# Both output projections of a two-layer decoder as seven half-size products per 1024-row chunk

## The chip, the cores and the metric

The kernel runs on one core of a Trainium2 chip. The metric is the device time of one execution in microseconds; the median of three runs of the kernel before is 1294.98 us (1292.8 to 1294.99).

## What is computed

Input and output are 1024 rows by 1024 columns of float32. The first (even) layer has two head groups, a gated linear recurrence (A, the RG-LRU) and stick-breaking attention (B). Their gated outputs stand side by side, 2048 columns, and go through one output projection. The second (odd) layer is sliding-window attention with an output projection of 1024 columns. Each layer ends with a layer norm over the residual:

```python
y = jnp.concatenate([y_a, y_b], axis=-1)              # even layer: 1024 x 2048
return jnp.einsum('bse,ed->bsd', y, w_out)            # 2048 -> 1024; odd layer: 1024 -> 1024
...
x = _layer_norm(DEEPNORM_ALPHA * x + y, ln_g[li], ln_b[li])
```

## The kernel before

Every float32 product is made of three matmuls in a reduced float32 type: both operands are split into a high and a low part, and high by high, high by low and low by high are added in PSUM (`mm3`, L109 to L112). One matmul takes a 128x128 block of the left side and moves 512 columns; PSUM holds eight banks of 128x512.

**Order.** A static scheduler fixes the order of instructions on each engine's queue when the program is built. Within a queue an instruction that waits holds up all that stand behind it; this includes SP's queue, which issues nearly all DMAs, and POOL's.

**Stages.** Even layer: attention heads with projections as filler, then the recurrence (RG-LRU, eight blocks `f`), in whose gaps the even output projection starts on the attention half of `y`; then the projection alone; then layer norm of each 128-row tile, transposes of the new `x` (`x1tr`, L626), and the odd layer's input projections (`pj_ok`, `pj_ov`, `pj_oq`, `pj_og`), its attention (`opv` is the last product of a head pair), its output projection, and the final layer norm with the stores.

**The output projection** (`out_proj`) goes over two column halves `dm`. For each it takes the pieces `e` of the contraction (16 in the even layer, 8 in the odd one, 128 rows of weight each), and for each piece the eight row tiles `s`; all eight banks accumulate at once (`ope`, `opo`). A piece is 24 matmuls. In the second half the last eight pieces run row tile by row tile, so that a row's layer norm goes beside the next row's 24 matmuls. In all there are 768 matmuls in the even layer and 384 in the odd one (its last row tile is cut in two column halves).

**Operands.** A weight piece comes by one 256 KB DMA into one of three buffers `wr`; POOL makes its high part (`wh`, L102) and its low part (`wl`, L103). Each tile of `y`, 128x1024, is split once: ACT or POOL makes the high part (L592, L590), DVE the low part (L593).

**Residual.** `xpre` holds the input rows; DVE's L492 adds a finished bank into it, L495 takes statistics. The load of `gb` (L580, 1 MB) and the eight loads of `xpre` (L582, 512 KB each) go into memory that the recurrence uses until its last product `ya` (L442).

**Layer norm.** Even: L500, L501, L505, L529 on small tiles, L531 on ACT, L532 on POOL, L537 on DVE, then the transposes with their splits L118 (ACT) and L119 (DVE). Odd: all on DVE (L500, L505, L519, L523), but for the last row.

## Time and profile before

| | |
|---|---|
| median of the three runs | 1294.98 us |
| span of the profiled execution | 1294.7 us |
| PE matmul busy | 1259.2 us (97%) |
| DVE busy | 792.5 us (61%) |
| ACT busy | 563.7 us (44%) |
| POOL busy | 566.5 us (44%) |
| instructions on PE, DVE, POOL | 6656, 1693, 695 |
| DMA | 64.15 MB, mean 50 GB/s |

Matmuls are pipelined, so the busy time of one (about 0.39 us at the full clock) is longer than the distance between the starts of two; the distance is what a matmul costs. Within a page of rows, the square bracket after an instruction is the idle time of its engine before it and what ended that.

### The profile page before, as it was taken

Reading aid. Unit: us, or ns where it says so; the run is one execution under the profiler, and the core shown is the slowest. Engines: PE = TensorE matmul, PEld = TensorE weight load, DVE = VectorE, ACT = ScalarE, POOL = GpSimd, SP = SyncE. Lnnn points to the kernel's source line nnn. Section 1 sums busy time; section 2 is a strip of 40 time slices with the busy share of each in tenths; the row PEclk is TensorE's granted clock in tenths of the full one; section 3 lists DMA queues with packets and bytes.
Section 4 is the critical chain, followed back from the end, with each engine's and each line's share of the span. In section 5 each row is a group of like instructions: output and inputs, shape, how many; then the busy total and the mean of one; then the engine's idle time right before and its main releaser. Section 6 shows DMA issues by size and latency. Waiting matters only on the chain.

```text
span 1294.7 us, 18487 instructions
## 1 busy us (share of the span) xinstructions
PE 1259.2 (97%) x6656; PEld 1077.1 (83%) x6656; DVE 792.5 (61%) x1693; ACT 563.7 (44%) x1219; POOL 566.5 (44%) x695
## 2 busy tenths in 40 slices
PE   7999999999999999999998899999999999999997
PEld 6988988898889888888776688888788888887886
DVE  6266455645564559577777931126457877778467
ACT  4134333333333335565556700013357777778400
POOL 0332243314322422556657763536445555556440
PEclk9999999999999999999999899999899999999999
DMA  6211011101110110111111052210111111111122
GB/s 204 58 41 33 25 49 34 33 17 50 33 34 24 50 37 13 37 46 46 44 49 41 25 219 64 70 29 26 49 33 33 34 34 34 33 34 40 35 90 98
DMA packets 33643, 64.15 MB, mean 50 GB/s; under 512 B 3984, under 2 KB 5392, under 8 KB 33296
## 3 DMA queue, kind: packets, MB, share of 16 engines
q1 hardware_dynamic: 32976, 61.92, 15.8%
q8 instruction: 53, 0.87, 0.3%
q10 hardware_dynamic: 576, 1.05, 0.3%
q14 instruction: 38, 0.31, 0.1%
...
## 4 chain that ended last, share of the span: by engine, by line
PE 80%; DVE 11%; ACT 4%; issue 3%; POOL 1%; DMA 1%; POOLq 0%; ACTq 0%; DVEq 0%
PE ope L110 4%; PE ope L112 4%; PE ope L111 4%; PE tr L283 2%; PE pjv L112 2%; PE pjv L111 2%; PE pjv L110 2%; PE pj_g L112 2%; PE pj_g L110 2%; PE pj_g L111 2%; PE pj_q L110 2%; PE pj_q L111 2%; PE pj_q L112 2%; PE pj_k L111 2%; PE pj_k L112 2%
## 5 line engine op out<-in xcount | busy, mean ns | idle before, releaser
L264 ACT ACTIVATE C<-z 128x512 f32<-128x512 f32 (+3 forms) x96 | 47.4, 494 | 130.2 <-DVE z L261 77.0
L756 POOL TENSOR_SCALAR S<-S,sm 128x256 f32<-128x256 f32 (+1 forms) x128 | 59.9, 482 | 77.8 <-DVE sm L754 30.0
L751 ACT ACTIVATE S<-S,sm 128x256 f32<-128x256 f32 (+1 forms) x128 | 62.6, 490 | 57.1 <-DVE sm L747 55.3
L501 ACT ACTIVATE rs<-mv,eps_t 128x1 f32<-128x1 f32 x16 | 4.7, 295 | 183.4 <-DVE mv L500 183.4
L492 DVE SCALAR_TENSOR_TENSOR xpre<-xpre,ope 128x512 f32<-128x512 f32 x16 | 10.8, 681 | 107.0 <-PE ope L112 107.0
L110 PE MATMUL pjv<-wh_v,xh 128*128 128x256 f32 x256 | 73.3, 286 | 0.0
L112 PE MATMUL pjv<-wh_v,xl 128*128 128x256 f32 x256 | 72.4, 283 | 0.0
L111 PE MATMUL pjv<-wl_v,xh 128*128 128x256 f32 x256 | 72.4, 283 | 0.0
L312 POOL TENSOR_TENSOR yb<-pvt,yb 128x128 f32<-128x128 f32 x32 | 15.8, 492 | 126.2 <-DVE pvt L311 110.0
L273 DVE TENSOR_TENSOR_SCAN C<-C,C,one 128x512 f32<-128x512 f32 x32 | 41.7, 1302 | 41.7 <-ACT C L264 41.7
L273 DVE TENSOR_TENSOR_SCAN C<-C,one 128x512 f32<-128x512 f32 (+1 forms) x64 | 54.7, 854 | 16.4 <-ACT C L264 16.3
L118 ACT CAST wt<-tr 128x512 fp32r<-128x512 f32 (+3 forms) x96 | 46.6, 486 | 40.7 <-PE tr L283 38.9
L275 DVE TENSOR_TENSOR B<-B,C 128x512 f32<-128x512 f32 (+3 forms) x96 | 57.3, 597 | 10.2 <-ACT pvt L309 0.5
L261 DVE TENSOR_TENSOR z<-z,mask 128x128 f32<-128x128 f32 x64 | 18.8, 296 | 67.6 <-PE z L259 65.7
L102 POOL TENSOR_SCALAR wh_g<-wr_g 128x512 fp32r<-128x512 f32 x16 | 10.7, 668 | 111.3 <-PE pjv L112 42.6
L110 PE MATMUL pj_k<-xh,wh_k 128*128 128x512 f32 x128 | 52.7, 412 | 5.6 <-DVE wh_k L105 5.6
L119 DVE TENSOR_TENSOR wt<-tr,wt 128x512 fp32r<-128x512 f32 (+3 forms) x96 | 52.6, 549 | 7.9 <-ACT wt L118 7.6
L110 PE MATMUL pj_ag<-xh,wh_ag 128*128 128x512 f32 x128 | 51.8, 405 | 5.7 <-DVE xc L381 5.7
L110 PE MATMUL ope<-wh_e,yhb 128*128 128x512 f32 x128 | 51.2, 403 | 6.2 <-DVE gg L395 3.8
L110 PE MATMUL pj_oq<-x1h,wh_oq 128*128 128x512 f32 x128 | 52.8, 412 | 0.0
L111 PE MATMUL pj_k<-xl,wh_k 128*128 128x512 f32 x128 | 51.2, 400 | 1.3 <-DVE xl L133 1.3
L110 PE MATMUL pj_q<-xh,wh_q 128*128 128x512 f32 x128 | 52.0, 406 | 0.1
...
## 6 DMA issues: line engine op xcount, KB each, us to landing
...
```

The lines of the kernel that those rows point to most:

```text
L110: nc.tensor.matmul(ps, wh, xh, start=start, stop=False)
L111: nc.tensor.matmul(ps, wh, xl, start=False, stop=False)
L112: nc.tensor.matmul(ps, wl, xh, start=False, stop=stop)
L118: nc.scalar.copy(h, ps)
L119: nc.vector.tensor_tensor(out=l, in0=ps, in1=h.bitcast(F32), op=ALU.subtract)
L261: nc.vector.tensor_tensor(out=z[:, W - P:W], in0=z[:, W - P:W], in1=mask, op=ALU.add)
L264: nc.scalar.activation(C[:, :W], z[:, :W], AF.Sigmoid, scale=-SC)
L273: nc.vector.tensor_tensor_scan(cr, cr, one.broadcast_to([P, W]), init, ALU.mult, ALU.mult)
L275: nc.vector.tensor_tensor(out=B[:, :W], in0=B[:, :W], in1=C[:, 1:W + 1], op=ALU.mult)
L283: nc.tensor.transpose(tr[:, t * P:(t + 1) * P], B[:, t * P:(t + 1) * P], ident)
L751: nc.scalar.activation(Sb[:, j, lo:], Sb[:, j, lo:], AF.Exp, bias=nm[:, j:j + 1], accum_out=den[:, j:j + 1])
L756: nc.gpsimd.tensor_scalar(out=Sb[:, j, lo:], in0=Sb[:, j, lo:], scalar1=rec[:, j:j + 1], scalar2=0.0, op0=ALU.mult, op1=ALU.add)
```

## The change

`out_proj` gives way to `fast_out`. The contraction is cut into chunks of 1024 (even: the attention half first, then the recurrence half; odd: one). Each chunk is a 2x2 block product with blocks of 512, done as seven block products instead of eight (a Strassen form). A product is four row tiles by four 128-row pieces by three, 48 matmuls, in four banks; two sets of four banks alternate (X and Y). P0 is A11 by B11 (X), P1 A12 by B21 (Y), P2 S2 by T2 (added on P0's banks), P3 S1 by T1 (Y), P4 S3 by T3 (X), P5 S4 by B22 (on Y), P6 A22 by T4 (on X).

DVE adds each product into one to three quarters of `xpre` (`add_to`, L502 and L504 of the new file). The sums S of quarters of `y` are formed by DVE (L571), the sums T of weight quarters by POOL (L571), from weights that are loaded again for each product (L593). Splits are made per product and per 128x512 tile, one product ahead in the program text: `y` high on ACT (L622), low on DVE (L623), weight high on ACT (L626; before on POOL), weight low on POOL (L627). The last chunk's P5 finishes row tiles 0 to 3, and P6 finishes 4 to 7, each followed by its layer norm; the cut of the last odd row goes away. L549 and L554 are the old L532 and L537. PE's queue holds 6086 matmul and transpose rows against 6252.

```diff
+    XB = ["pj", "pj", "pj", "pv"]
+    YB_ = ["z", "z", "tr", "tr"]
 
     LNC = 768
 
-    def out_proj(w_src, es, yh, n_tail, tail_piece, lnp, gb, after, name, final):
+    PRODUCTS = [("A11", "B11", 0, True), ("A12", "B21", 1, True), ("S2", "T2", 0, False), ("S1", "T1", 1, True),
+                ("S3", "T3", 0, True), ("S4", "B22", 1, False), ("A22", "T4", 0, False)]
+    def fast_out(w_src, chunks, lnp, wtmp, wop, gb, after, name, final, first_by_rows):
...
+        def add_to(half, dm, p, ps, cols=(0, HALF)):
+            s = half * 4 + p
             c0, c1 = cols
             xt = xpre[:, s, dm * HALF + c0:dm * HALF + c1]
+            if (s, dm, c0) in touched or (s, dm, 0) in touched:
+                nc.vector.tensor_tensor(out=xt, in0=ps[:, c0:c1], in1=xt, op=ALU.add)
+            else:
+                nc.vector.scalar_tensor_tensor(out=xt, in0=xt, scalar=ALPHA, in1=ps[:, c0:c1],
+                                               op0=ALU.mult, op1=ALU.add)
+            touched.add((s, dm, c0))
...
+            def y_raw(op, t):
+                if op in ("A11", "A12", "A22"):
+                    return {"A11": A11, "A12": A12, "A22": A22}[op][t]
+                if op == "S2":
+                    if "S2" not in hold:
+                        hold["S2"] = half_tiles(f"S2{pre}")
+                    tt(nc.vector, A11[t], A11[t], A21[t], ALU.subtract)
+                    tt(nc.vector, hold["S2"][t], A22[t], A11[t], ALU.subtract)
+                    return hold["S2"][t]
+                if op == "S1":
+                    tt(nc.vector, A21[t], A21[t], A22[t], ALU.add)
+                    return A21[t]
+                if op == "S3":
+                    return A11[t]
+                if op == "S4":
+                    tt(nc.vector, A12[t], A12[t], hold["S2"][t], ALU.subtract)
+                    return A12[t]
+            def w_load(j, k, t, nm):
+                raw = wpool.tile([P, HALF], F32, tag="wr", name=f"wr_{nm}{pre}_{t}", bufs=3)
+                nc.sync.dma_start(raw, w_src[j, e0 + 4 * k + t])
+                return raw
+            def w_raw(op, t):
+                if op in ("B11", "B21", "B22"):
+                    return w_load(int(op[2]) - 1, int(op[1]) - 1, t, op)
+                if op == "T2":
+                    if "T2" not in hold:
+                        hold["T2"], hold["T3"] = half_tiles(f"T2{pre}"), half_tiles(f"T3{pre}")
+                    b22, b12 = w_load(1, 1, t, "c"), w_load(1, 0, t, "d")
+                    tt(nc.gpsimd, hold["T3"][t], b22, b12, ALU.subtract)
+                    b11 = w_load(0, 0, t, "e")
+                    tt(nc.gpsimd, hold["T2"][t], hold["T3"][t], b11, ALU.add)
+                    return hold["T2"][t]
+                if op == "T3":
+                    return hold["T3"][t]
+                if op == "T1":
+                    b12, b11 = w_load(1, 0, t, "f"), w_load(0, 0, t, "g")
+                    tt(nc.gpsimd, b12, b12, b11, ALU.subtract)
+                    return b12
...
+            def make(i, t):
+                yop, w_op = PRODUCTS[i][:2]
+                r = y_raw(yop, t)
+                yo_ = slot(f"yo{pre}{i}_{t}", F32R)
+                nc.scalar.copy(yo_[:, 0, :], r)
+                nc.vector.tensor_tensor(out=yo_[:, 1, :], in0=r, in1=yo_[:, 0, :].bitcast(F32), op=ALU.subtract)
+                r = w_raw(w_op, t)
+                wh, wl = wop(f"{pre}{i}_{t}")
+                nc.scalar.copy(wh, r)
+                nc.gpsimd.tensor_tensor(out=wl, in0=r, in1=wh.bitcast(F32), op=ALU.subtract)
+                return yo_, wh, wl
...
+        def mm(ps, ops, p, t, start, stop, c0=0, c1=HALF):
+            yo_, wh, wl = ops
+            c = slice(p * P, (p + 1) * P)
+            f = partial(nc.tensor.matmul, skip_group_check=True)
+            f(ps[:, c0:c1], yo_[:, 0, c], wh[:, c0:c1], start=start, stop=False)
+            f(ps[:, c0:c1], yo_[:, 0, c], wl[:, c0:c1], start=False, stop=False)
+            f(ps[:, c0:c1], yo_[:, 1, c], wh[:, c0:c1], start=False, stop=stop)
...
+        prep(0)
+        for k, (ci, i) in enumerate(steps):
+            prep(k + 1)
+            ops = made.pop(k)
...
+            if last and i >= 5:
+                half = i - 5
+                for p in range(4):
+                    s = half * 4 + p
+                    b = ps[xy, p]
+                    for t in range(4):
+                        mm(b, ops[t], p, t, False, t == 3)
+                    dm = 1 - half
+                    add_to(half, dm, p, b)
+                    stat(s, dm, 0, HALF)
+                    mr = ln_a(s)
+                    if pend is not None:
+                        ln_c(pend)
+                    ln_b(s, *mr)
+                    pend = s
                 continue
+            if fresh:
+                for p in range(4):
+                    ps[xy, p] = bank(tags[p], f"fo{name}{ci}_{i}_{p}")
+            rows = first_by_rows and k == 0
+            order_ = [(p, t) for p in range(4) for t in range(4)] if rows else \
+                [(p, t) for t in range(4) for p in range(4)]
+            for p, t in order_:
+                mm(ps[xy, p], ops[t], p, t, fresh and t == 0, t == 3)
+            for p in range(4):
+                b = ps[xy, p]
+                for half, dm in ([(0, 0)], [(0, 0)], [(0, 1), (1, 0), (1, 1)], [(1, 1)], [(1, 1)],
+                                 [(0, 1)], [(1, 0)])[i]:
+                    add_to(half, dm, p, b)
+                    if last and ((i == 1) or (i == 4)):
+                        stat(half * 4 + p, dm, 0, HALF)
...
+    def wop_pool(nm):
+        return (wpool.tile([P, HALF], F32R, tag="wh", name=f"wh_{nm}", bufs=5),
+                wpool.tile([P, HALF], F32R, tag="wl", name=f"wl_{nm}", bufs=5))
+    fast_out(w_even_out, [([ytile["b", n] for n in range(8)], 8), ([ytile["a", f] for f in range(8)], 0)],
+             lnp, None, wop_pool, gb, after_even, "e", False, False)
...
+    def wop_slot(nm):
+        hl = slot(f"whl_{nm}", F32R)
+        return hl[:, 0, :], hl[:, 1, :]
+    fast_out(w_odd_out, [([ytile["o", p] for p in range(8)], 0)], ep, None, wop_slot, gb2, after_odd, "o", True, True)
```

Three places show how the order moves. The first is SP's queue at the end of the recurrence. Before, three weight pieces of the even projection, then the loads of `gb` and `xpre`, then the next piece:

```order
L93 DMA wr_e_0_7258<-in_w_even_out_dram 128x512
L93 DMA wr_e_1_7288<-in_w_even_out_dram 128x512
L93 DMA wr_e_2_7318<-in_w_even_out_dram 128x512
L580 DMA gb<-in_e_ln_dram 128x2048
L582 DMA xpre<-in_x_dram 128x1024 x8
L93 DMA wr_e_3_7348<-in_w_even_out_dram 128x512
```

Now (the letters c, d, e are the three quarters of which T3 and T2 are formed, f and g those of T1; the digit is the 128-row piece):

```order
L593 DMA wr_ee_1_7108<-in_w_even_out_dram 128x512
L593 DMA wr_ce_2_7120<-in_w_even_out_dram 128x512
L593 DMA wr_de_2_7122<-in_w_even_out_dram 128x512
L693 DMA gb<-in_e_ln_dram 128x2048
L695 DMA xpre<-in_x_dram 128x1024 x8
L593 DMA wr_ee_2_7125<-in_w_even_out_dram 128x512
L593 DMA wr_ce_3_7137<-in_w_even_out_dram 128x512
L593 DMA wr_de_3_7139<-in_w_even_out_dram 128x512
L593 DMA wr_ee_3_7142<-in_w_even_out_dram 128x512
L593 DMA wr_fe_0_7209<-in_w_even_out_dram 128x512
L593 DMA wr_ge_0_7211<-in_w_even_out_dram 128x512
```

The third load of piece 2 of T2 now stands behind the nine loads, and with it all of piece 3 and T1. The second place is POOL's queue over the same weights. Before, each piece is one copy and one subtraction:

```order
L102 TENSOR_SCALAR wh_e_3_7350<-wr_e_3_7348 128x512
L103 TENSOR_TENSOR wl_e_3_7351<-wr_e_3_7348,wh_e_3_7350 128x512
L102 TENSOR_SCALAR wh_e_4_7380<-wr_e_4_7378 128x512
L103 TENSOR_TENSOR wl_e_4_7381<-wr_e_4_7378,wh_e_4_7380 128x512
L102 TENSOR_SCALAR wh_e_5_7410<-wr_e_5_7408 128x512
```

Now, for the products P2 (T2) and P3 (T1, which is formed in the tile wr_fe):

```order
L627 TENSOR_TENSOR wl_e_1_7112<-T2e_7082,wh_e_1_7111 128x512
L571 TENSOR_TENSOR T3e_7085<-wr_ce_2_7120,wr_de_2_7122 128x512
L571 TENSOR_TENSOR T2e_7083<-T3e_7085,wr_ee_2_7125 128x512
L571 TENSOR_TENSOR T3e_7085<-wr_ce_3_7137,wr_de_3_7139 128x512
L571 TENSOR_TENSOR T2e_7083<-T3e_7085,wr_ee_3_7142 128x512
L571 TENSOR_TENSOR wr_fe_0_7209<-wr_fe_0_7209,wr_ge_0_7211 128x512
L627 TENSOR_TENSOR wl_e_2_7129<-T2e_7083,wh_e_2_7128 128x512
L627 TENSOR_TENSOR wl_e_3_7146<-T2e_7083,wh_e_3_7145 128x512
```

The low part of P2's piece 2 now stands behind the sums of piece 3 and the first sum of T1. The third place is the end of the even projection, on POOL. Before, five rows' L532 stand behind the last weight piece in one group:

```order
L102 TENSOR_SCALAR wh_e_7_7803<-wr_e_7_7801 128x512
L103 TENSOR_TENSOR wl_e_7_7804<-wr_e_7_7801,wh_e_7_7803 128x512
L532 TENSOR_TENSOR xpre<-xpre,gb 128x1024 x5
L102 TENSOR_SCALAR whl_ok_8175<-wr_ok_8173 128x512
L102 TENSOR_SCALAR whl_ok_8180<-wr_ok_8178 128x512
```

Now, with the weights of the last product P6 (T4, formed in T2's tiles):

```order
L627 TENSOR_TENSOR wl_e_0_8206<-T2e_7776,wh_e_0_8205 128x512
L571 TENSOR_TENSOR T2e_7777<-wr_he_3_8232,T2e_7777 128x512
L549 TENSOR_TENSOR xpre<-xpre,gb 128x1024 x2
L627 TENSOR_TENSOR wl_e_1_8216<-T2e_7776,wh_e_1_8215 128x512
L627 TENSOR_TENSOR wl_e_2_8226<-T2e_7777,wh_e_2_8225 128x512
L627 TENSOR_TENSOR wl_e_3_8236<-T2e_7777,wh_e_3_8235 128x512
L549 TENSOR_TENSOR xpre<-xpre,gb 128x1024 x2
```

Two rows' L549 now stand ahead of the low parts of three of the four pieces of the last product.

## Rows read from the trace of the kernel before

**Rows 1.** Busy time of each engine in stretches, granted clock, DMA share.

```profile
core 0: us, PE busy (x) PEld busy (x) DVE busy (x) ACT busy (x) POOL busy (x), PEclk, DMA share, GB/s
...
720.00:740.00 20.00, 15.15 (x50) 11.58 (x51) 20.00 (x15) 15.99 (x18) 14.06 (x9) 0.83 0.13 41
740.00:905.00 165.00, 165.00 (x746) 136.97 (x745) 53.35 (x83) 20.82 (x29) 84.44 (x70) 1.00 0.25 80
...
1215.00:1275.00 60.00, 59.73 (x266) 49.46 (x267) 35.13 (x62) 4.54 (x9) 22.46 (x24) 1.00 0.22 71
```

**Rows 2.** Timeline of PE: start, duration, instruction; the odd layer's first projections.

```profile
911.98 0.80 PE L110 MATMUL pj_ov<-x1h,whl_ov 128*128 128x512 f32 x1 [1.87 <-POOL whl_ov L102]
...
914.28 0.63 PE L110 MATMUL pj_oq<-x1h,wh_oq 128*128 128x512 f32 x1
914.71 0.63 PE L111 MATMUL pj_oq<-x1l,wh_oq 128*128 128x512 f32 x1
```

**Rows 3.** Timelines of DVE, SP and POOL at the end of the recurrence.

```profile
754.00 0.92 DVE L442 TENSOR_TENSOR ya<-xc,gg 128x512 f32<-128x512 f32 x1
...
755.00 0.33 SPq L580 DMA_DIRECT2D gb<-in_e_ln_dram  x1
...
760.84 0.33 SPq L93 DMA_DIRECT2D wr_e<-in_w_even_out_dram  x1
...
771.91 0.62 POOL L102 TENSOR_SCALAR wh_e<-wr_e 128x512 fp32r<-128x512 f32 x1 [11.07 <-DMA wr_e<-in_w_even_out_dram]
```

**Rows 4.** Groups by line, POOL 700 and DVE 740 to 905 us: busy, mean ns, idle.

```profile
L532 POOL TENSOR_TENSOR xpre<-xpre,gb 128x1024 f32<-128x1024 f32 x7 | 16.9, 2411 | 21.7 <-ACT xpre L531 21.6
...
L495 DVE BATCH_NORM_STATS2 ste<-xpre 128x6 f32<-128x512 f32 x16 | 10.8, 687 | 0.2
L492 DVE SCALAR_TENSOR_TENSOR xpre<-xpre,ope 128x512 f32<-128x512 f32 x16 | 10.8, 681 | 107.0 <-PE ope L112 107.0
L537 DVE TENSOR_TENSOR xpre<-xpre,gb 128x1024 f32<-128x1024 f32 x7 | 9.0, 1280 | 0.1
L119 DVE TENSOR_TENSOR x1l<-x1tr,x1h 128x512 fp32r<-128x512 f32 x8 | 5.3, 668 | 0.0
L593 DVE TENSOR_TENSOR yhla<-ya,yhla 128x1024 fp32r<-128x1024 f32 x1 | 1.2, 1211 | 0.0
```

**Rows 5.** Timeline of POOL in the undisturbed stretch of the even projection.

```profile
819.93 1.29 POOL L103 TENSOR_TENSOR wl_e<-wr_e,wh_e 128x512 fp32r<-128x512 f32 x1
...
823.95 0.62 POOL L102 TENSOR_SCALAR whl_e<-wr_e 128x512 fp32r<-128x512 f32 x1 [0.46 <-DMA wr_e<-in_w_even_out_dram]
```

**Rows 6.** Timeline of SP: the load into the buffer freed at 821.22 us.

```profile
821.25 5.04 SPq L93 DMA_DIRECT2D wr_e<-in_w_even_out_dram  x3
```

**Rows 7.** Timeline of DVE, end of the even projection: additions of three of eight rows.

```profile
864.95 0.69 DVE L492 SCALAR_TENSOR_TENSOR xpre<-xpre,ope 128x512 f32<-128x512 f32 x1 [1.48 <-PE ope L112]
870.39 0.69 DVE L492 SCALAR_TENSOR_TENSOR xpre<-xpre,ope 128x512 f32<-128x512 f32 x1 [1.84 <-PE ope L112]
...
901.18 0.69 DVE L492 SCALAR_TENSOR_TENSOR xpre<-xpre,ope 128x512 f32<-128x512 f32 x1 [2.33 <-PE ope L112]
```

**Rows 8.** Timeline of PE: the last product of the odd attention.

```profile
1219.86 0.28 PE L787 MATMUL opv<-ptl,VP 128*128 128x256 f32 x1
```

**Rows 9.** Timeline of DVE: additions of two rows before the final layer norm, last instruction.

```profile
1255.14 0.68 DVE L492 SCALAR_TENSOR_TENSOR xpre<-xpre,opo 128x512 f32<-128x512 f32 x1
...
1259.68 0.68 DVE L492 SCALAR_TENSOR_TENSOR xpre<-xpre,opo 128x512 f32<-128x512 f32 x1
...
1290.35 0.96 DVE L523 SCALAR_TENSOR_TENSOR xpre<-xpre,rs,gb 128x384 f32<-128x384 f32 x1
```

**Rows 10.** Timelines of POOL and DVE in the recurrence, where both read SBUF tiles.

```profile
719.04 1.71 POOL L103 TENSOR_TENSOR wl_e<-wr_e,wh_e 128x512 fp32r<-128x512 f32 x1
720.72 1.59 POOL L102 TENSOR_SCALAR wh_e<-wr_e 128x512 fp32r<-128x512 f32 x1
...
719.54 2.28 DVE L593 TENSOR_TENSOR ylb<-yb,yhb 128x1024 fp32r<-128x1024 f32 x1
```

108 lines of the change are left out of this document (33 added, 75 removed).

## The prediction

> **What bounds the kernel now.** I read the windows by stage first. From 740 to 905 us, the even output projection, PE is busy all the time at the full clock, DVE a third of it; from 1215 to 1275 us, the odd one, PE is busy for 59.73 of 60 us [rows 1]. The cost of a matmul at the full clock is read from the row tiles at the end of the even projection: 24 matmuls between two additions that wait for PE, 5.44 us, 0.2267 each [rows 7]. At the half clock, which PE showed after 1.87 us of idling, two matmuls start 0.43 us apart [rows 2]. So in both projections the number of matmuls sets the time, and whoever takes matmuls away gains, as long as operands come in time. Third, the places where PE could starve. At the end of the recurrence DVE is the full engine (20.00 of 20 us, PE 15.15) [rows 1], and a weight piece behind the loads of `gb` and `xpre` keeps POOL waiting for 11.07 us [rows 3]. PE doesn't feel that, because it has pieces in hand. At the ends of the two layers, DVE and POOL follow the last matmuls [rows 7, 9].
>
> **Matmuls removed.** Seven products of 48 instead of eight: 48 matmuls per chunk, three chunks. Even: 96 x 0.2267 = -21.8 us; odd: 48 x 0.2267 = -10.9 us [rows 7]. That is -32.7 us if nothing else moves.
>
> **Start of the even projection.** Call L the end of the recurrence's last product, 754.92 us [rows 3]. By then PE had done some 133 of the 768 `ope` matmuls: from L to the last row's addition at 901.18 [rows 7] it was never idle [rows 1]; 146.3 us hold 645 matmuls, less some ten for the transposes that stand between. In the new order P0, P1 and two pieces of P2 can be done by L: 120, much the same. But the third load of P2's piece 2 stands behind the loads of `gb` and `xpre` on SP, where before stood a piece that PE didn't need yet. These loads can't start before L (755.00), and what is behind them reached POOL at 771.91, L + 17.0 [rows 3]. Then POOL's queue: the T2 sum of piece 2 (1.29 us, a subtraction's time [rows 5]) to L + 18.3; T3 of piece 3 to L + 19.6; the load of its third quarter into the buffer freed at L + 18.3, which takes 2.73 us (a buffer freed at 821.22 was used at 823.95 [rows 5, 6]), to L + 21.0; T2 of piece 3 to L + 22.3; the two loads of T1 into buffers freed at L + 19.6, to L + 22.4; T1 to L + 23.7; and only then the low part of piece 2, to L + 25.0. PE stands from about L to L + 25.0. With the 13 matmuls by which it is behind (2.9) and one piece of 12 at the half clock (12 x 0.20 = 2.4) it lags by 30.3. L itself can move: DVE, the full engine, makes fewer splits of `y` before L (six of 1.21 less would be 7 us [rows 4]), but sums S come in. Bounds -1 and +7, I take 2.5 us earlier. Term: **+27.8** (20 to 32).
>
> **Operands in the other products.** Before, POOL worked one copy and one subtraction (L102 0.62, L103 1.29 [rows 5]) per 24 matmuls, 1.91 us in 5.44. Now a piece feeds 12 matmuls, 2.72 us. A plain piece needs one subtraction, 1.29, and is covered. A piece of T2 needs three operations, 3.87 us, and three loads in three buffers, so that from one T3 to the next at least 1.29 + 2.73 = 4.02 us pass; a piece of T1 has two loads and the same 4.02. For the eight pieces that is 8 x (4.1 - 2.72) = 11 us of PE waiting if nothing was made ahead, and 0 if all was. In the second even chunk some can be made during P0 and P1, where POOL needs half of the time: I take 6. The same banks serve P6 of one chunk and P0 of the next, so that PE waits for additions (0.68 each [rows 4]): 1. Term: **+7** (2 to 12).
>
> **End of the even layer.** On POOL two L549, 2.41 us each [rows 4], now stand ahead of the low parts of three pieces of P6, the last product: +3 (2 to 5). Since these pieces come last, the four rows 4 to 7 end together, where before a row ended every 5.44 us and its layer norm lay beside the next one's matmuls. Before, the first `pj_ov` matmul came 10.8 us after the last row's addition [rows 2, 7]. Now DVE has, from the last matmul to that point, 4 additions (2.7), 4 statistics (2.8), 12 transposed splits (8.0), 5 final additions L554 (6.4) [rows 4], and a dozen instructions of a few columns, between 0 and half of a 128x512 one each (0 to 4, I take 3): 22.9, and with the first transposes and ACT's casts 24.1. The projections `pj_ok` lie in it before and after. +13.3 (5 if the rows still end one by one, to 16). Even layer in all: -21.8 + 27.8 + 7 + 3 + 13.3 = **+29**.
>
> **Odd layer.** The last attention product ends at 1220.1 [rows 8]. Before, 294 matmuls were left, covered by PE alone. Now 24 of P0 and P1 and five products are left, 264, 59.8 us of PE. The sums of T2 need slots that P0 gives free: POOL starts on them at about 1223. Nothing is made ahead here, so T2 and T1 go at their own pace: 8 x 4.1 = 33 us, 1256; the last low part and 12 matmuls, 1260; P4 (10.9), 1271. From there DVE sets the end: P4's additions and statistics and some splits stand ahead, 4 x (0.68 + 0.69) + 2 = 7.5 [rows 4]; then eight rows' layer norm. A row costs DVE 4.54 us back to back (1255.14 to 1259.68 [rows 9]); before, most of the eight lay beside 5.44 us of matmuls each, now a row has only 12 matmuls (2.72), and the eight take 8 x 4.54 = 36.3. After DVE's last instruction (1291.31 [rows 9]) 3.4 us of stores follow. End: 1271 + 7.5 + 36.3 + 3.4 = 1318, against 1294.7: **+23.5**, the 10.9 us of removed matmuls included. Lower bound: no wait for operands, P4 ends at 1220 + 168 x 0.2267 = 1258, additions hidden but for 2.7: 1258 + 2.7 + 36.3 + 3.4 = 1300.5, +6. Upper: POOL at the contended times of [rows 10], +30. POOL's and ACT's split instructions for P0 and P1 also stand among the last attention heads' steps, which can move the attention's end by -3 to +10; I take 0.
>
> **Sum.** 1294.7 + 29 + 23.5 = 1347.2 us of span; the median is 0.3 above the span. Forecast 1347.5 us. All lower ends give 1294.7 + 7 + 3 = 1305, all upper ones 1294.7 + 43 + 40 = 1378.
>
> **Rivals.**
> 1. *POOL and DVE exclude each other.* In the recurrence a POOL subtraction began at 719.04 and took 1.71; DVE's split began at 719.54 and took 2.28 instead of 1.21, ending 1.07 after POOL's end; POOL's copy, begun at 720.72, took 1.59 instead of 0.62, that is until 0.5 after DVE's end [rows 4, 10]. They went one after the other. A chunk now has 44 POOL operations (44 x 1.29 = 56.8) and 44 DVE ones from SBUF (half of 1.21 to 0.68, 28.6): 85.4 us one after the other, against 336 x 0.2267 = 76.1 of PE. In the first chunk +9, in the second +4 beyond my 6, and a T2 piece of the odd chunk at 5.2 instead of 4.1, 4 x 1.1: +17, 1364.5 us. Against it: both engines have slack in the plain products, and T2's pace is set by loads that no engine delays. The Trainium skill (SBUF — State Buffer, "SBUF: two separate sides") has this as a rule: the port pair that the two share is an exclusive lock, held for a whole instruction by whichever starts first, for DVE instructions with two SBUF inputs. The rows above agree.
> 2. *Only the start costs.* P2's and P3's sums run ahead of PE in the second chunk and the odd layer, and the last even rows end one by one: -21.8 + 27.8 + 2 + 2 + 5 = +15, odd +6: 1316 us.
> 3. *Faster.* The recurrence ends early enough. DVE and POOL are its full engines, and the change takes copies off POOL (to ACT) and whole-tile splits off DVE. If L came 20 us sooner, the start's term would be 10; with every other cost at its lower end, -21.8 + 10 + 2 + 2 + 5 = -3, odd +6 - 3: 1295 us. It decides from 23 us on, and at 30 would give 1285. For it: DVE has no free time there [rows 1]. Against: six splits fewer are 7 us, and the gates' chain remains.
> 4. *The removal doesn't take place.* PE's queue is 166 rows shorter; I give it nothing.
>
> **How the numbers follow.** Forecast (1325 to 1357) 0.56; rival 1 and other upper ends (above 1357) 0.16; rival 2 (1298 to 1325) 0.20; within 0.2%, about what a measurement of this kernel tells from no change, 0.02; faster 0.06. So slower 0.92. The range 1306 to 1368 leaves out faster and same (0.08), some 0.06 of rival 2 and 0.06 above.
>
> **What would show it.** Right: PE stands still for 20 us or more in one piece just after the loads of `gb` and `xpre`, POOL waits there for the piece behind them; in the last even product four rows' additions follow each other on DVE; in the odd layer POOL's T2 sums come every 4 to 5 us with PE waiting for them, and DVE has no gap from P4 to the end. The start is wrong if PE's longest gap there is under 15 us; the odd term is wrong if P4 ends before 1262 us less the shift of what stands ahead; all is wrong if the second even chunk and both ends run at PE's pace of 2.72 us a piece.

## The result, and the profile after

The changed kernel takes 1359.89 us (median of four runs, 1359.33 to 1361.2); the kernel before took 1294.04 us beside it (1292.8 to 1294.99). The ratio is 1.0515, with a 95% interval of 1.050 to 1.053: slower by 5%. The profiled execution has a span of 1357.6 us against 1294.7. Two single runs among the experiments, one of the two of e5 and one of the eight of e8, took some 80 us more than the same kernel's others and are left out. Times are medians of a kernel's runs (of two for most experiments); landmarks inside the span come from one profiled execution. The length of a product runs from the start of the first of its 48 matmuls to the start of the next product's first, counted in PE's order.

The page of the changed kernel, its first part (busy time, share of the span, instructions) and, from the second, PE and its granted clock in 40 slices of 33.9 us:

```profile
PE 1248.7 (92%) x6488; PEld 1056.3 (78%) x6488; DVE 943.7 (70%) x1876; ACT 637.7 (47%) x1368; POOL 650.1 (48%) x724
...
PE   8999999999999999999996399797999999998793
...
PEclk9999999999999999999999699897999999998897
```

PE carries out fewer matmuls and has lost its full share in slices 22 and 23 (713 to 781 us, the start of the even projection), 26 (848 to 882, its second chunk), 28 (916 to 950, the end of the even layer), and 37, 38 and 40 (the odd projection and the end). DVE is now busy for 943.7 us, before for 792.5. The windows that answer to [rows 1], with the busy time of each engine and the instructions in brackets:

```profile
core 0: us, PE busy (x) PEld busy (x) DVE busy (x) ACT busy (x) POOL busy (x), PEclk, DMA share, GB/s
720.00:740.00 20.00, 16.00 (x61) 12.54 (x62) 20.00 (x20) 10.79 (x14) 13.09 (x8) 0.91 0.19 54
740.00:786.00 46.00, 18.79 (x53) 13.81 (x52) 34.42 (x37) 16.29 (x29) 24.40 (x15) 0.63 0.56 200
...
832.00:922.00 90.00, 78.53 (x336) 63.33 (x334) 63.19 (x83) 29.71 (x51) 66.36 (x44) 0.94 0.32 97
922.00:950.00 28.00, 18.49 (x77) 13.52 (x77) 25.94 (x38) 13.26 (x22) 20.01 (x13) 0.76 0.09 29
...
1263.00:1312.00 49.00, 39.26 (x146) 27.90 (x147) 40.98 (x45) 17.64 (x32) 38.19 (x26) 0.93 0.41 128
1312.00:1357.00 45.00, 21.81 (x96) 17.52 (x94) 42.07 (x79) 8.20 (x17) 14.70 (x11) 0.78 0.31 111
```

Between 740 and 905 us PE was never idle before [rows 1]. Now it gets through 53 matmuls in the 46 us to 786, where the full pitch of 0.2267 us would have given 203.

| landmark, us | before | after | difference |
|---|---|---|---|
| recurrence's last product ends (L) | 754.92 | 751.67 | -3.3 |
| last row's addition / last even matmul ends | 901.2 | 921.9 | +20.7 |
| first `pj_ov` matmul | 911.98 | 949.96 | +38.0 |
| last attention product | 1220.1 | 1257.4 | +37.3 |
| end of the span | 1294.7 | 1357.6 | +62.9 |

**Start of the even projection.** PE's gaps (the idle time before an instruction and its releaser stand in the square bracket), then POOL's queue, SP's, and a row of DVE's in the same stretch:

```profile
758.74 0.77 PE L635 MATMUL foe<-wh_e,yoe 128*128 128x512 f32 x1 [17.79 <-DVE xpre L504]
771.39 2.07 PE L635 MATMUL foe<-wh_e,yoe 128*128 128x512 f32 x4 [4.41 <-ACT wh_e L626]
778.48 0.79 PE L636 MATMUL foe<-wl_e,yoe 128*128 128x512 f32 x1 [5.02 <-POOL wl_e L627]
```
```profile
751.09 1.71 POOL L571 TENSOR_TENSOR T3e<-wr_ce,wr_de 128x512 f32<-128x512 f32 x1
767.55 3.14 POOL L571 TENSOR_TENSOR T2e<-T3e,wr_ee 128x512 f32<-128x512 f32 x1 [14.75 <-DMA wr_ee<-in_w_even_out_dram]
770.65 1.26 POOL L571 TENSOR_TENSOR T3e<-wr_ce,wr_de 128x512 f32<-128x512 f32 x1
773.29 1.26 POOL L571 TENSOR_TENSOR T2e<-T3e,wr_ee 128x512 f32<-128x512 f32 x1 [1.38 <-DMA wr_ee<-in_w_even_out_dram]
775.49 1.27 POOL L571 TENSOR_TENSOR wr_fe<-wr_fe,wr_ge 128x512 f32<-128x512 f32 x1 [0.94 <-DMA wr_ge<-in_w_even_out_dram]
776.71 3.40 POOL L627 TENSOR_TENSOR wl_e<-T2e,wh_e 128x512 fp32r<-128x512 f32 x2
```
```profile
751.75 0.33 SPq L693 DMA_DIRECT2D gb<-in_e_ln_dram  x1
752.17 4.48 SPq L695 DMA_DIRECT2D xpre<-in_x_dram  x8
757.85 0.33 SPq L593 DMA_DIRECT2D wr_ee<-in_w_even_out_dram  x1
```
```profile
764.07 5.50 DVE L623 TENSOR_TENSOR yoe<-yb,yoe 128x512 fp32r<-128x512 f32 x9
```

The loads of `gb` and `xpre` leave right after L. The third quarter of P2's piece 2 (`wr_ee`) stands behind them and reaches POOL at L + 15.9, where 17.0 had been worked out from [rows 3]. Then comes the queue that the prediction wrote down: T2, T3, T2, T1 and only then the low part of piece 2. It begins at 776.71, L + 25.0; the prediction had its end there. PE has it at 778.48, L + 26.8. The main cause is the first T2 sum, 3.14 us instead of 1.29: DVE's splits follow each other every 0.60 us until 769.57, and the sum ends 1.1 us behind the last of them. What else the prediction had otherwise is the first gap. It let pieces 0 and 1 of P2 run before L. P2 accumulates on P0's banks, P0's additions into `xpre` wait for the loads of `xpre`, and so these pieces too came after them; PE stood from 740.95, before L.

**Second even chunk, its P2.** POOL's rows, one of SP's, then PE's two longest gaps:

```profile
856.60 1.68 POOL L571 TENSOR_TENSOR T3e<-wr_ce,wr_de 128x512 f32<-128x512 f32 x1 [1.72 <-DVE yoe L623]
858.36 1.60 POOL L571 TENSOR_TENSOR T2e<-T3e,wr_ee 128x512 f32<-128x512 f32 x1
861.87 1.60 POOL L571 TENSOR_TENSOR T3e<-wr_ce,wr_de 128x512 f32<-128x512 f32 x1 [1.90 <-DMA wr_de<-in_w_even_out_dram]
863.54 1.59 POOL L571 TENSOR_TENSOR T2e<-T3e,wr_ee 128x512 f32<-128x512 f32 x1
867.15 1.46 POOL L571 TENSOR_TENSOR wr_fe<-wr_fe,wr_ge 128x512 f32<-128x512 f32 x1 [2.02 <-DMA wr_ge<-in_w_even_out_dram]
868.57 1.71 POOL L627 TENSOR_TENSOR wl_e<-T2e,wh_e 128x512 fp32r<-128x512 f32 x1
```
```profile
858.69 0.43 SPq L593 DMA_DIRECT2D wr_de<-in_w_even_out_dram  x1
```
```profile
861.89 1.19 PE L635 MATMUL foe<-wh_e,yoe 128*128 128x512 f32 x4 [2.87 <-ACT wh_e L626]
870.33 0.80 PE L636 MATMUL foe<-wl_e,yoe 128*128 128x512 f32 x1 [7.25 <-POOL wl_e L627]
```

From one T3 to the next it is 861.87 - 856.60 = 5.27 us. The prediction had 4.02 at least: a sum of 1.29 and a load of 2.73. The sum took 1.68, 0.39 more, as the others take 1.6 here where a subtraction alone took 1.29 [rows 5]. The larger part, 0.86, is the load: T3 needs two quarters, both leave when T3's end frees their buffers (858.31 and 858.69), and the second could be used 3.59 us after that end. P2 took 23.0 us instead of 10.88. (The expectations of e4 and e7 give 22.4 for it, some three matmuls too few.)

**End of the even layer.** DVE's and POOL's rows from the last matmuls on, and the first projection matmul of the odd layer:

```profile
920.11 3.38 DVE L554 TENSOR_TENSOR xpre<-xpre,gb 128x1024 f32<-128x1024 f32 x1 [2.38 <-POOL xpre L549]
...
937.51 3.41 DVE L554 TENSOR_TENSOR xpre<-xpre,gb 128x1024 f32<-128x1024 f32 x1 [1.35 <-POOL xpre L549]
...
943.67 3.42 DVE L554 TENSOR_TENSOR xpre<-xpre,gb 128x1024 f32<-128x1024 f32 x2
```
```profile
935.03 4.80 POOL L549 TENSOR_TENSOR xpre<-xpre,gb 128x1024 f32<-128x1024 f32 x2 [7.99 <-ACT xpre L548]
...
945.97 3.34 POOL L549 TENSOR_TENSOR xpre<-xpre,gb 128x1024 f32<-128x1024 f32 x1
```
```profile
949.96 0.50 PE L110 MATMUL pj_ov<-x1h,whl_ov 128*128 128x512 f32 x1
```

From the last matmul (921.9) to `pj_ov` it takes 28.1 us, before 10.8 [rows 2, 7]. L554 cost 1.28 in [rows 4]; beside POOL the four shown took 3.4, 3.4 and twice 1.7. POOL's last layer norm products come as late as 935 to 949, because the four rows end together.

**Odd projection.** POOL's and DVE's queues while P3 ends and P4 runs, and DVE from there to its last instruction:

```profile
1299.11 6.95 POOL L627 TENSOR_TENSOR whl_o<-T3o,whl_o 128x512 fp32r<-128x512 f32 x4
1306.02 6.93 POOL L627 TENSOR_TENSOR whl_o<-wr_B22o,whl_o 128x512 fp32r<-128x512 f32 x4
```
```profile
1306.03 7.47 DVE L623 TENSOR_TENSOR yoo<-yo,yoo 128x512 fp32r<-128x512 f32 x5
```
```profile
1303.00:1354.00 51.00, 30.81 (x136) 24.96 (x134) 50.97 (x89) 11.93 (x24) 23.01 (x16) 0.84 0.29 101
```

P4 ends at 1311.7, which is 54.4 us after the attention's last product; the prediction had 51. One load was not priced: that of the odd layer norm's constants (1 MB) leaves on SP at 1261.07, ahead of a quarter of T2's second piece at 1262.99, and POOL has that quarter only at 1269.41, 6.4 us later. The two columns that matter in the last row are the third (DVE, 50.97 of 51 us) and the first (PE, 30.81): after P4 DVE alone sets the end, as forecast.

### The profile page after: what moved, and what is told of

Same layout as the page of the kernel before. It is cut to its first block, busy times and chain, and to the rows that moved or that the text cites. A ratio compares the mean times of both kernels' runs of the same rounds, so it can differ in the third digit from the quotient of the medians.

```text
span 1357.6 us, 18732 instructions
## 1 busy us (share of the span) xinstructions
PE 1248.7 (92%) x6488; PEld 1056.3 (78%) x6488; DVE 943.7 (70%) x1876; ACT 637.7 (47%) x1368; POOL 650.1 (48%) x724
## 4 chain that ended last, share of the span: by engine, by line
PE 65%; DVE 17%; POOL 6%; ACT 4%; DMA 3%; issue 3%; POOLq 0%; SPq 0%; ACTq 0%; DVEq 0%
PE tr L283 2%; PE pjv L112 2%; PE pjv L110 2%; PE pjv L111 2%; PE pj_g L112 2%; PE pj_oq L110 2%; PE pj_g L110 2%; PE pj_oq L112 2%; PE pj_oq L111 2%; PE pj_g L111 2%; PE pj_q L110 2%; PE pj_q L112 2%; PE pj_q L111 2%; PE pj_k L111 2%; PE pj_k L112 2%
## 5 line engine op out<-in xcount | busy, mean ns | idle before, releaser
L635 PE MATMUL foe<-wh_e,yoe 128*128 128x512 f32 x224 | 82.8, 410 | 30.8 <-DVE xpre L504 17.8
L264 ACT ACTIVATE C<-z 128x512 f32<-128x512 f32 (+3 forms) x96 | 47.5, 495 | 130.2 <-DVE z L261 77.0
L636 PE MATMUL foe<-wl_e,yoe 128*128 128x512 f32 x224 | 91.5, 409 | 14.4 <-POOL wl_e L627 14.4
L842 POOL TENSOR_SCALAR S<-S,sm 128x256 f32<-128x256 f32 (+1 forms) x128 | 58.8, 474 | 78.7 <-DVE sm L840 33.6
L637 PE MATMUL foe<-wh_e,yoe 128*128 128x512 f32 x224 | 90.2, 405 | 0.0
L635 PEld LDWEIGHTS foe<-wh_e,yoe 128*128 128x128 f32 x224 | 43.7, 197 | 43.4 <-issue 20.1
L273 DVE TENSOR_TENSOR_SCAN C<-C,C,one 128x512 f32<-128x512 f32 x32 | 41.7, 1303 | 41.7 <-ACT C L264 41.7
L636 PEld LDWEIGHTS foe<-wl_e,yoe 128*128 128x128 f32 x224 | 44.6, 199 | 25.7 <-POOL wl_e L627 16.4
L275 DVE TENSOR_TENSOR B<-B,C 128x512 f32<-128x512 f32 (+3 forms) x96 | 57.4, 597 | 10.2 <-ACT pvt L309 0.5
L102 POOL TENSOR_SCALAR wh_g<-wr_g 128x512 fp32r<-128x512 f32 x16 | 10.7, 666 | 110.4 <-PE pjv L112 42.5
L502 DVE TENSOR_TENSOR xpre<-foe,xpre 128x512 f32<-128x512 f32 x56 | 36.5, 683 | 33.7 <-PE foe L637 33.2
```

The lines of the kernel that those rows point to most:

```text
L264: nc.scalar.activation(C[:, :W], z[:, :W], AF.Sigmoid, scale=-SC)
L273: nc.vector.tensor_tensor_scan(cr, cr, one.broadcast_to([P, W]), init, ALU.mult, ALU.mult)
L275: nc.vector.tensor_tensor(out=B[:, :W], in0=B[:, :W], in1=C[:, 1:W + 1], op=ALU.mult)
L635: f(ps[:, c0:c1], yo_[:, 0, c], wh[:, c0:c1], start=start, stop=False)
L636: f(ps[:, c0:c1], yo_[:, 0, c], wl[:, c0:c1], start=False, stop=False)
L637: f(ps[:, c0:c1], yo_[:, 1, c], wh[:, c0:c1], start=False, stop=stop)
```

## The experiments

Kernels e1 to e7 are edits of the changed kernel, e8 and e9 rearrange its even part, e10 and e11 are edits of the kernel before. Line numbers of an edited kernel are shifted by a few.

**e1: the even layer in the new form, the odd one in the old.** `out_proj` stands beside `fast_out`, and only the call at the odd layer's end changes:

```diff
-    fast_out(w_odd_out, [([ytile["o", p] for p in range(8)], 0)], ep, None, wop_slot, gb2, after_odd, "o", True, True)
+    out_proj(w_odd_out, list(range(8)), yh_odd, 8, lambda ti, src, nm: load_piece(src, nm, pool=slots),
+             ep, gb2, after_odd, "o", True)
```

> The even projection in the new form, the odd one as before. My theory, that the two projections cost separately: the even one ends 38.0 us later than before in the changed kernel's trace (first pj_ov product 911.98 before, 949.97 after), so about 1294 + 38 = 1332 us. Rival, that the costs are shared (for instance the odd layer's attention pays for what the even one leaves behind): more than 3 us away from 1332.

Measured: 1333.15 us, ratio 1.0309 (1.0279 to 1.0339). The two layers' costs add up: the odd one costs 1359.9 - 1333.2 = 26.7 us (predicted 23.5), the even one the rest, some 40 (predicted 29). 1333.15 lies 1.2 us from the 1332 of the expectation.

**e2: the odd layer's sums T from six buffers of their own**, so that no load waits for a buffer:

```diff
-                raw = wpool.tile([P, HALF], F32, tag="wr", name=f"wr_{nm}{pre}_{t}", bufs=3)
+                if final and nm in "cdefgh":
+                    raw = lnp.tile([P, HALF], F32, tag="wr2", name=f"wr_{nm}{pre}_{t}", bufs=6)
+                else:
+                    raw = wpool.tile([P, HALF], F32, tag="wr", name=f"wr_{nm}{pre}_{t}", bufs=3)
```

> The changed kernel, but the odd projection's quarters for T2, T1 and T4 are loaded into six buffers of their own instead of the three shared ones. Theory (three buffers and the load's way into them set the pace of T2 and T1): the eight pieces of P2 and P3, 37.9 us from 1263.7 to 1301.5 us in the changed kernel, fall to about 30, and the kernel gains 4 to 8 us, less than the pieces do, because DVE has work of its own there. Rival (POOL and DVE exclude each other, POOL's own time sets the pace): pieces stay above 35 us, the kernel gains under 2 us.

Measured: 1359.93 us, ratio 1.0516 (1.0479 to 1.0552): no gain. The waits for loads did go. P2 and P3 together took 33.6 us instead of 37.2 (the expectations have 37.9, up to P3's last matmul, with four of P4's in between). But see what POOL and DVE did in the meantime (timeline of e2, POOL first, then DVE):

```profile
1272.95 3.43 POOL L571 TENSOR_TENSOR T3o<-wr_co,wr_do 128x512 f32<-128x512 f32 x2
1276.34 3.42 POOL L571 TENSOR_TENSOR T2o<-T3o,wr_eo 128x512 f32<-128x512 f32 x2
```
```profile
1273.46 3.46 DVE L571 TENSOR_TENSOR S2o<-yo,yo 128x512 f32<-128x512 f32 x2
1276.85 3.46 DVE L571 TENSOR_TENSOR yo<-yo,S2o 128x512 f32<-128x512 f32 x2
```

Neither engine idles, and each needs 1.7 us for an operation of two SBUF inputs: one of POOL, one of DVE, one of POOL. DVE's splits for P4 came later, P4 took 16 us instead of 10.9, and the gain was gone. My theory named the loads as what sets T2's pace; they were one of two limits that lay over each other.

**e3: the even layer's loads in the order of their need.** The quarter of `xpre` that P0 adds into goes first on SP (1 MB), the other 3 MB (`rest`) go on ACT's queue, and `gb` comes after the first chunk's last weights:

```diff
-    nc.sync.dma_start(gb, ...)
-    for s in range(NS):
-        nc.sync.dma_start(xpre[:, s, :], x[s * P:(s + 1) * P, :])
+    for s in range(4):
+        nc.sync.dma_start(xpre[:, s, 0:HALF], x[s * P:(s + 1) * P, 0:HALF])
...
+            if k == 1 and not final:
+                rest()
+            if k == 5 and not final:
+                load_gb(wdma[0, 'B22', 3])
```

> The changed kernel, but of the residual only the quarter that P0 and P1 are added to is loaded on SP ahead of the weights (1 MB); the other 3 MB go by ACT's queue, and the layer norm's constants (1 MB) after the first chunk. Theory (what stands still at the start are the 5 MB ahead of the weights on SP): the third load of T2's piece 2 reaches POOL 6 to 10 us after the end of the recurrence instead of 15.9, P3 of the first chunk ends 5 to 12 us earlier, the kernel gains as much. Rival (POOL's queue of sums, 44 operations a chunk, is the cause): under 2 us.

Measured: 1354.96 us, ratio 1.0477 (1.0447 to 1.0508); the span is 4.6 us shorter than that of the changed kernel and `pj_ov` comes 5.3 us earlier. POOL's wait, which was 14.75 us:

```profile
760.76 1.42 POOL L572 TENSOR_TENSOR T2e<-T3e,wr_ee 128x512 f32<-128x512 f32 x1 [7.69 <-DMA wr_ee<-in_w_even_out_dram]
```

This is L + 10.2 instead of L + 15.9, and the 5 us arrive at the end of the span. The three marks of the theory (6 to 10 us to POOL, P3's end and the kernel 5 to 12 us earlier) are each missed by a little, the last two with 4.9; the rival, under 2 us, is out. So the loads ahead of the weights are a cause of the start's cost, though not all of it: PE's first gap is still 15.75 us.

**e4: the low part of `y` isn't made.** In both projections the third matmul uses the high part instead, so that DVE does 84 operations less:

```diff
-                nc.vector.tensor_tensor(out=yo_[:, 1, :], in0=r, in1=yo_[:, 0, :].bitcast(F32), op=ALU.subtract)
...
-            f(ps[:, c0:c1], yo_[:, 1, c], wh[:, c0:c1], start=False, stop=stop)
+            f(ps[:, c0:c1], yo_[:, 0, c], wh[:, c0:c1], start=False, stop=stop)
```

> The changed kernel without the splits that make the low part of y in both projections; the third matmul takes the high part again, so PE's work is the same and the result is not the reference's. DVE loses 84 instructions with two SBUF inputs, 51 us at 0.61 each. Theory (loads and queue order): POOL's operations get back to about 1.29 us, but the waits of P2 in the second even chunk (22.4 us for 48 matmuls) and of the odd P2 and P3 (37.9 us) stay within 3 us of that; the kernel gains 6 to 12 us, nearly all at the odd end, where DVE is full. Rival (exclusion of POOL and DVE sets these waits): both fall by 4 us or more, the kernel gains 18 us or more.

Measured: 1336.47 us, ratio 1.0334 (1.0304 to 1.0364), 23.4 us less. POOL's subtractions were back to 1.29 us wherever DVE had no sum beside them. In the places that the expectation names, less happened than the rival said: P2 of the second chunk took 3.3 us less (19.7; the theory had allowed 3), P2 and P3 of the odd layer 0.6 less (36.6). But the gain is far beyond the 6 to 12 us of the theory, and most of it lies elsewhere than at the odd end. L comes at 742.04, 9.6 us earlier, since DVE is the full engine of the recurrence [rows 1], and the splits for P0 and P1 stand in its queue there. The windows row of e4 for the recurrence's end shows DVE (third column) at 14.48 of 20 us, where it had been 20.00:

```profile
720.00:740.00 20.00, 16.21 (x59) 12.28 (x59) 14.48 (x13) 14.24 (x18) 11.29 (x9) 0.87 0.22 69
```

`pj_ov` is 14.7 us earlier, the attention's end 19.5 us. This bears on the prediction's third rival: L does move when DVE has less to do, but 9.6 us is what leaving out all these splits gives, and the rival needs 23.

**e5: e2 and e4 together** (diffs as above).

> The two edits of e2 and e4 together: the odd projection's quarters in six buffers of their own, and no low part of y (the high part is used twice, so the result is not the reference's). Theory (two limits of nearly the same height lie over each other in the odd projection: the load into three buffers, and the time in which POOL and DVE keep each other out; taking away one shows the other): with both gone the eight pieces of P2 and P3 go at POOL's own pace, 4 x 3.87 + 4 x 2.58 = 26 us, so 26 to 30 us after 37.9 in the changed kernel, 33.6 in e2 and 36.4 in e4, and the time is 4 to 9 us under e4's 1336.5. Rival (the buffers matter nowhere, as e2's time alone says): within 2 us of e4's.

Measured: 1331.42 us, 5.1 less than e4. In the odd layer P2 and P3 take 31.6 us, not the 26 to 30 expected; P2 to P4 take 42.5 us. The changed kernel took 48.1 for P2 to P4, e2 49.5, e4 47.5. Either remedy alone gives 0.6 us or nothing, both give 5.6. That is the mark of two limits one behind the other: loads into three buffers, and DVE's splits. POOL's row for the same two sums that took 3.42 us in e2:

```profile
1256.44 2.48 POOL L571 TENSOR_TENSOR T2o<-T3o,wr_eo 128x512 f32<-128x512 f32 x2
```

DVE has nothing to do there, and POOL needs 1.2 us a sum. So the two engines do hold each other up. How much of the 5.6 us is that, and how much the splits' own time in DVE's queue, these runs don't separate: without the splits both are gone.

**e6: the second half of every odd row's layer norm on ACT and POOL**, as the last row has it already:

```diff
-            if final and s == NS - 1:
+            if final:
+                cut = LNC if s == NS - 1 else HALF
...
-                edges = (0, LNC // 2, LNC) if s == NS - 1 else (0, 512, 1024)
+                edges = (0, LNC // 2, LNC) if s == NS - 1 else (0, HALF)
```

> The changed kernel, but the second half of each row tile's last layer norm goes by ACT and POOL, as that of the last row's end did already. DVE's work per row falls from 4.54 to 3.1 us. Theory (from the end of P4 on DVE alone sets the end, 45.2 us): the end comes 3 to 9 us sooner; nearer 4 if POOL's two products per row (1.29 each) keep DVE's with two SBUF inputs out, nearer 9 if they run side by side. Rival (the stores or PE set the end): under 1 us.

Measured: 1361.98 us, ratio 1.0536 (1.0506 to 1.0567), no gain; from P4's end to the span's end 45.9 us, before 45.8 (the expectation has 45.2). DVE has 14 operations of 0.74 us fewer and seven of one column more, and from P4's end to its last instruction it idles for 0.07 us in all; POOL ends 1.8 us behind it. So neither the stores nor PE set the end. Its remaining operations beside POOL (timeline of e6, DVE, then POOL):

```profile
1343.00 0.74 DVE L541 SCALAR_TENSOR_TENSOR xpre<-xpre,rs,gb 128x512 f32<-128x512 f32 x1
1343.66 1.75 DVE L537 SCALAR_TENSOR_TENSOR xpre<-xpre,mv,gb 128x512 f32<-128x512 f32 x1
...
1346.65 1.76 DVE L541 SCALAR_TENSOR_TENSOR xpre<-xpre,rs,gb 128x512 f32<-128x512 f32 x1
```
```profile
1343.14 1.72 POOL L532 TENSOR_TENSOR xpre<-xpre,gb 128x512 f32<-128x512 f32 x1
1344.82 1.71 POOL L531 TENSOR_TENSOR xpre<-xpre,gb 128x512 f32<-128x512 f32 x1
```

An operation that DVE hands to POOL comes back as one that DVE waits out.

**e7: the other way round, all sums T on DVE** (the same edit at T3, T2, T1 and T4):

```diff
-                    tt(nc.gpsimd, hold["T3"][t], b22, b12, ALU.subtract)
+                    tt(nc.vector, hold["T3"][t], b22, b12, ALU.subtract)
...
```

> The changed kernel, but the sums T of weight quarters are formed by DVE (0.61 us each undisturbed) instead of POOL (1.29): 48 operations move. Theory (POOL and DVE exclude each other, so what counts is the sum of both, 85 us a chunk): the sum falls by 16 x 0.68 = 11 us a chunk, P2 of the second even chunk falls from 22.4 to under 18 us, the odd P2 to P4 (48.7 us) to under 44, and the kernel gains 5 to 15 us. Rival (each engine has its own limit, and DVE is the fuller one in the recurrence and at the odd end): the kernel loses 2 to 10 us, since DVE gets 29 us more.

Measured: 1371.7 us, ratio 1.0611 (1.0577 to 1.0646), 11.8 us more. A sum on DVE takes 0.68 us instead of POOL's 1.29, so that the two engines' time added up falls; yet P2 of the second chunk takes 23.8 us (23.0), P3 13.2 (11.1), P3 of the first chunk 22.2 (10.9), and the odd layer from P4's end on 49.7 (45.8), where T4's sums now stand in the queue of the engine that sets the end. The theory that the two engines' time added up is the bound fell, and the loss is past the rival's 2 to 10 us: which queue a sum stands in counts for more.

**e8: the fast chunk between two old ones.** If the costs are those of a start and an end without cover, the fast products belong in the middle. The odd layer is old; in the even one the attention half's first column half runs in the old form (192 matmuls), then the recurrence half as seven products (336), then the attention half's second column half, row tile by row tile (192), with the layer norm beside it as before. 48 matmuls are saved.

```diff
-    fast_out(w_even_out, [([ytile["b", n] for n in range(8)], 8), ([ytile["a", f] for f in range(8)], 0)],
-             lnp, None, wop_pool, gb, after_even, "e", False, False)
+    fast_out(w_even_out, [([ytile["a", f] for f in range(8)], 0)],
+             lnp, None, wop_pool, gb, after_even, "e", False, False, ([ytile["b", n] for n in range(8)], yh_b))
```

> A version made to keep the gain: the odd projection as before; in the even one the attention half of the contraction in the old form (its first column half ahead, its second, row tile by row tile, at the end, so that the layer norm lies beside 24 matmuls a row as before), and only the recurrence half as seven products, between the two. 48 matmuls fewer than before, 10.9 us. Theory (the losses are the loads at the start, the sums' pace and the bare layer norms): the first and third are gone, since 192 matmuls of the old form cover the loads and the end is the old one; the second stays in part. Time 1284 to 1294 us. If the exclusion of POOL and DVE (85 us a chunk against 76 of PE) is the bound of the chunk wherever it stands, 1292 to 1298.

Measured: 1292.86 us, ratio 0.9995 (0.9983 to 1.0007): no change, and in the range of both expectations. The seven products took 93.0 us, where 384 old matmuls take 87.0: P0 to P3 60 us instead of 43.5.

**e9: e8 with the loads split.** The column half of `xpre` that is added into first (2 MB) goes ahead; the other half goes behind P2's second sum, `gb` behind the loads for P5:

```diff
-        nc.sync.dma_start(xpre[:, s, :], x[s * P:(s + 1) * P, :])
+        nc.sync.dma_start(xpre[:, s, 0:HALF], x[s * P:(s + 1) * P, 0:HALF])
...
+            if hyb and k == 2:
+                rest(wdma[0, 'e', 1])
+            if hyb and k == 5:
+                load_gb(wdma[0, 'B22', 3])
```

> e8 with the loads in the order of need: ahead of the chunk's weights only the first column half of the residual (2 MB), its second half after the second piece of T2, the layer norm's constants after the products' plain weights. In e8 PE stood for 3.0 us and then worked at the half clock at the start of the chunk, and P0 to P3 took 60 us (765.1 to 825.2) against 43.5 of matmuls. Theory (in e8 the loads at the start still cost 5 to 8 us, and the sums' pace the rest): P0 and P1 fall from 32.9 us to 22 to 27, the time to 1284 to 1290 us. Rival (the pace of sums and splits bounds the chunk wherever it starts): P2 and P3 grow by what P0 and P1 lose, 1291 to 1294 us.

Measured: 1286.94 us, ratio 0.9954 (0.9940 to 0.9967), 0.46% faster than the kernel before. P0 and P1 took 26.0 us, in the range expected. It looks like a late success of the seven products. But the chunk took 86.9 us, no less than the old 87.0. The windows row of e9 over most of it (its length, then PE, PEld, DVE, ACT, POOL, the clock, DMA):

```profile
765.00:852.00 87.00, 79.77 (x338) 62.22 (x337) 69.60 (x78) 28.27 (x49) 69.96 (x52) 1.00 0.47 151
```

And of the kernel before, over its 384 matmuls there:

```profile
765.00:853.00 88.00, 88.00 (x390) 72.88 (x389) 9.71 (x16) 0.00 (x0) 38.12 (x40) 1.00 0.28 88
```

Fewer matmuls fill the same time (338 in 87 us, before 390 in 88); DVE and POOL are busy for 70 us each, before for 10 and 38. P4, P5 and P6 run at PE's pace (10.88 us each), P0 to P3 take 54.3 (26.0 and 28.2) instead of 43.5: the 10.9 us that were saved are spent there. So the gain had to be checked for its source.

**e10: the kernel before with e9's loads.**

```diff
                 wh, wl = load_piece(w_src[dm, e], f"{name}{dm}_{e}")
+                if not final and dm == 0 and idx == 11:
+                    rest(last_w['x'])
+                if not final and dm == 0 and idx == 14:
+                    load_gb(last_w['x'])
```

> The kernel before, all matmuls in the old form, with the loads of e9: half of xpre first, the other half after the twelfth weight piece, gb after the fifteenth. Theory (in the old form PE has pieces in hand and feels neither the loads nor their order; e9's gain is that of the 48 matmuls taken away): 1291 to 1296 us, within 0.2% of the kernel before; the first pj_ov matmul at 910 to 914 us, as before (911.98). Rival (e9's gain comes from the order of the loads, not from the products): 1284 to 1290 us, about -0.5%, pj_ov near 905.

Measured: 1293.95 us, ratio 1.0003 (0.9994 to 1.0012): the loads alone give nothing in the old form. The first `pj_ov` came at 909.53, and the stretch from the 192nd matmul to it took 145.15 us, as in the kernel before.

**e11: the kernel before with e9's loads and e9's order**, the attention half last, all products old:

```diff
+            if not final and dm == 1:
+                es = es[8:] + es[:8]
             nt = n_tail if dm == 1 else 0
```

> e10 with one more edit: in the second column half the recurrence pieces come first and the attention pieces last, row tile by row tile, which is the order of e9; all products in the old form. In e9 the stretch from the 192nd matmul to the first pj_ov took 141.3 us, in the kernel before and in e10 145.15 in both, while the 336 matmuls of e9's seven products took 86.9 us, no less than the 384 old ones (87.0). Theory A (the order and the row tiles' end give e9's gain, the seven products none): the stretch 141 to 143 us, the time 1287 to 1290 us. Theory B (the seven products give it, by what they leave undone on POOL and DVE before the end): the stretch 144.5 to 146 us, the time 1291 to 1296 us, as e10.

Measured: 1288.51 us, ratio 0.9961 (0.9949 to 0.9974). The intervals of e9 and e11 lie over each other. The stretch from the 192nd matmul to `pj_ov` took 141.75 us, as theory A said. So e9's gain is that of the order of the pieces (together with its loads; the order alone wasn't run), and the seven products gave nothing that these runs can tell. In [rows 2] PE waited 1.87 us for the weight of `pj_ov` and then ran at the half clock. The wait stands in e10 too, though there the granted clock stayed at 1.00 behind it. In e11 there is none (PE in e10, then POOL and PE in e11):

```profile
909.53 0.50 PE L117 MATMUL pj_ov<-x1h,whl_ov 128*128 128x512 f32 x1 [1.86 <-POOL whl_ov L109]
```
```profile
905.17 1.21 POOL L109 TENSOR_SCALAR whl_ov<-wr_ov 128x512 fp32r<-128x512 f32 x2
```
```profile
906.78 0.48 PE L117 MATMUL pj_ov<-x1h,whl_ov 128*128 128x512 f32 x1
```

POOL begins to split that weight 1.6 us before PE comes to it. With three short waits for transposes ahead of it, the wait makes up 2.6 of the 3.4 us by which the stretch is shorter. Why the attention half at the end makes the scheduler lay the transposes and POOL's work so that this wait goes wasn't followed up, and a version of e9 whose P0 to P3 keep PE's pace wasn't found or tried.

## Why the prediction came out as it did

Sign and mechanism were right, and 1359.89 lies within 1306 to 1368. It is 12.4 us above the forecast, 3 us inside the part (above 1357) that had been given to rival 1 and other upper ends. Of the 12.4, 9 come from the even layer, 2 from the odd one, and the rest from the attention's shift (-0.7) and from the median's lying 2.3 us above this span where I had put 0.3.

| step | predicted | measured |
|---|---|---|
| matmuls removed, even | -21.8 | as said: 10.88 us per 48 wherever PE doesn't wait |
| start of the even projection | +27.8 (20 to 32) | +30.2 |
| operands in the other products | +7 (2 to 12) | +14.5 |
| P6 behind two L549 | +3 (2 to 5) | +1.6 |
| end of the even layer | +13.3 (5 to 16) | +17.2 |
| odd layer | +23.5 (6 to 30) | +25.6 |

The terms measured for the even layer add up to 41.7, against the 38.0 of the landmark. The difference is mostly the 3.5 us that transposes took between the old matmuls from 786 to 901 us: in the new order they stand behind the last matmul and are counted in its end. The sum's +29 thus fell short in the start by 2.4, in the operands by 7.5 and in the end by 3.9, with these 3.5 and P6's 1.4 on the other side.

- **The start** came out nearly by the steps as written: the loads ahead, POOL's queue behind them, the low part of piece 2 done 1.8 us later than at L + 25.0, and L 3.3 us earlier (2.5 taken). P2 ends at 786.0; 144 even matmuls have begun by then, in the kernel before 277, so it is 133 x 0.2267 = 30.2 us behind. (By L the kernel before had begun 140, not some 133.) One step was wrong: pieces 0 and 1 of P2 were to be done before L, and waited for `xpre`. They then ran between two gaps, so that PE stood still for 17.8, 4.4 and 5.0 us, 27.2 in all, and not for 25 in one piece. My marks for this step were 20 us or more in one gap for right, under 15 for wrong; 17.8 is between them. e3 shows the loads as cause: with fewer of them ahead, 5 us come back.
- **Operands in the other products** was the term that was mis-sized, and past its upper bound. In the first chunk P3 to P6 lost 2.1 us, in the second P2 and P3 lost 12.3 (P2 23.0 us for 48 matmuls). I had put T2's period at 4.02 us or a little more; it was 5.27, for the second of T3's two loads (0.86) and for the sum's 1.68 us beside DVE's work (0.39). And I let some sums be made ahead during P0 and P1, which put the wait at 6 instead of 11; the low part of piece 2 stood behind T2 and T1 of the pieces after it, just as in the first chunk, and PE waited 7.25 us for it.
- **The end of the even layer** held what the prediction listed, but its L554 were counted at 1.28 us and took 1.7 to 3.4 beside POOL, and POOL itself came late (7.99 us of waiting for ACT).
- **The odd layer**: P4 ended 3.4 us later than worked out, and from there to the end it took 45.8 us, where the additions, layer norms and stores had been put at 47.2. DVE without a gap, and PE waiting for the T2 pieces, were both seen.
- **Rival 1** (POOL and DVE exclude each other, +17) was no rival but a part of the answer. Its rows stood in the document already [rows 10]; I judged that the slack in the plain products and the pace of the loads would hide it. The plain products of the first chunk showed that slack (P3 to P6 lost 2.1 us; the rival had said 9 for the chunk), the places with sums and both ends did not have it. Its size is known only roughly: leaving out DVE's splits gave 3.3 us of the 12.2 that the second chunk's P2 lost, and 0.6 in the odd P2 and P3 (e4). e2, e5 and e6 show it as a limit of its own: where loads no longer hold POOL back, the two engines hold each other up.
- **Rival 2** (only the start costs) failed by the second chunk and the end of the even layer. **Rival 3** (an earlier L makes it faster) failed by L: 3.3 us of the 23 that it needs. e4 shows what moves L, DVE's splits.
- **The expected gain** of 48 matmuls per chunk went into operands that aren't ready. Even where a fast chunk has old work on both sides (e9), 336 matmuls take as long as 384 (86.9 and 87.0 us).
